# Dilated attention on one NeuronCore: all key groups share one softmax scale before the value products, which then add up with features as rows

## The chip, the core and the metric

The kernel runs on one core of a Trainium2 chip. The core has a matrix engine, TensorE (called PE in the profile, with its weight loads as PEld), a vector engine (DVE), a scalar engine (ACT), GpSimd (POOL) and SyncE (SP), which here does nothing but issue DMAs. Each engine runs its own instructions in order, and semaphores hold an instruction until what it reads is there. The metric is the device time of one execution in microseconds (us).

## The reference, cut to what matters

The model has two layers over 512 tokens of width 1024. Layer 0 mixes latent attention and differential attention, layer 1 mixes dilated attention and stick-breaking attention; a gated convolutional feed-forward block follows each layer. The change lies in the dilated attention of layer 1. It has three groups of four heads of width 64; group g looks back at keys in steps of 1, 4 and 16 tokens. Each group has its own softmax, and the groups are merged by their softmax denominators:

```python
for g, (w, dil) in enumerate(((128, 1), (512, 4), (2048, 16))):
    s = q[g] @ k[g].T * scale - slope * steps          # only the keys of this group's steps
    m = max(s); e = exp(s - m); den = sum(e)
    outs.append((e / den) @ v[g]); lses.append(m + log(den))
wts = softmax(stack(lses), axis=groups)
o = sum_g wts[g] * outs[g]                             # then concatenated and @ w_out
```

Every matmul that feeds from a weight of the model is done as three fp32r products (high times high, high times low, low times high); scores, transposes and value products inside an attention are plain fp32.

## The kernel before, in words

P is 128 and S is 512; the tokens are NT = 4 tiles of 128, and ORDER walks them 3, 2, 1, 0. The function `odd` builds layer 1's mixer. Activations come in as xh and xl, features as rows, tokens as columns.

`proj_T` (the tile apt) makes a 128x512 slice of queries or keys, 24 matmuls of 512 columns (lines 263 to 265, the helper `mm3`), and its result is copied out of PSUM by ACT (L1101, queries) or DVE (L1103, keys). `proj_V` and its `tile_V(i)` (the tile apv) make the values of one token tile, 24 matmuls of 256 columns. Queries and keys of groups 1 and 2 are written in permuted order, so that the tokens of one residue modulo 4 are neighbours: these two groups then need keys of the same residue only, and are handled in four residues r of 128 tokens. Group 0 needs the token tile itself and the one before it.

The dilated attention of groups 1 and 2 is done in units (hp, rp), a pair of heads and a pair of residues. `score12` multiplies queries and keys into two PSUM banks (L1243, a 64-row half of the array for each of the two heads y), DVE adds the bias table and takes the extreme of each row (L1249), and ACT exponentiates and sums the row (L1253). `turn12` transposes the result through PE (L1265) and copies it back (L1267 on ACT, L1269 on DVE). `value12` takes the transposed probabilities as the stationary operand and 64 value columns as the moving one (L1282), and copies the sums, tokens as rows, into `ob` (L1286) with the row sum and the negated maximum beside them. When all units are done, sixteen DMAs (L1295) move `ob` into token order, as `on`.

Group 0 follows in units i of one token tile: `score0` (L1312, L1318, L1321), `turn0` (L1334, L1335, and from L1340 to L1348 the small DVE and ACT steps that turn the two pairs of row sum and maximum into two weights), `value0` (L1359, then L1363 to L1365: the two outputs times their weights, added) and `merged` (L1373: the merged tile is transposed back to features as rows, and split into high and low parts `oG` by L171 on ACT and L172 on DVE).

The helper `skewed` writes these stages one step apart, and puts a projection ahead of each step: the four `proj_T` of group 0 between the units of groups 1 and 2, the four `tile_V` between the units of group 0. The scheduler may then reorder what is written. After it comes the output projection (the tile ao, 24 matmuls of 512 columns for each token tile and the two transposes of normalised tiles, tp L211), whose order is fixed by `tc.manual_schedule`, and then the feed-forward block, which begins with the tile u.

`Weights` loads a weight of 512 KB through the SP queue (L50, tile wraw, three buffers) and splits it on ACT (L72) and DVE (L73). Its `depth` says how many units ahead it is split.

PSUM has eight banks, under five tags: "a" three, "s" two, and "t", "o", "n" one each.

## Time and profile before

| what | value |
|---|---|
| median of 3 runs | 1151.22 us (1151.09 to 1152.02) |
| the profiled execution | 1151.33 us, of which 1149.5 us are the span of the trace |
| PE busy | 1138.7 us |
| DVE busy, ACT busy | 805.6 us, 565.1 us |
| the stage that the change rewrites | from 707.7 us (after the stick-breaking values) to 767.5 us |
| output projection, then feed-forward | from 767.5 us, from 795.4 us |

Times within the trace are counted from the start of its span. A row of a group gives line, engine, operation, the tiles written and read, the shape, a count, the busy time and the mean length of one in ns, and the idle time before it. A row of the timeline gives the start, the length, and then the same names; matmuls are pipelined, so that the length of one overlaps the next and the distance from start to start is its price. Every plain fp32 matmul stands as two records, every fp32r matmul and every transpose as one.

### The profile page before, as it was taken

How to read it: one execution, taken by the hardware profiler on the slowest of the kernel's cores; microseconds unless marked ns; L12 is line 12 of the kernel's file. 1: busy time of each engine (PE TensorE's matmuls, PEld its weight loads, DVE VectorE, ACT ScalarE, POOL GpSimd, SP SyncE). 2: the span in 40 equal slices, each digit the busy share in tenths (PEclk: the TensorE clock that was granted, in tenths of full speed). 3: DMA queues.
4: the chain of work that ended last, by engine and by line, in shares of the span. 5: the costliest groups of instructions: out<-in, count | busy, mean ns of one | idle time of the engine just before them, and what ended most of it. 6: DMA issues, size and time to landing. Idle time of an engine off the chain costs nothing.

```text
span 1149.5 us, 15154 instructions
## 1 busy us (share of the span) xinstructions
PE 1138.7 (99%) x5668; PEld 939.3 (82%) x5668; DVE 805.6 (70%) x1389; ACT 565.1 (49%) x966; POOL 58.0 (5%) x139
## 2 busy tenths in 40 slices
PE   8999999999999999999999999999999999999997
PEld 7876777898888888888888877888988888888886
DVE  6677576467766767899874565577666666679896
ACT  5565566345444444457543464455533433445562
POOL 2100011210000000000030000003000000000002
PEclk9999999999999999999999999999999999999999
DMA  7320421143323332355736223323233323224461
GB/s 278 125 64 1 135 89 50 47 151 114 107 92 92 102 100 83 101 157 164 239 109 179 74 58 106 90 61 113 78 112 105 92 92 103 99 83 140 140 215 74
DMA packets 39050, 126.82 MB, mean 110 GB/s; under 512 B 4672, under 2 KB 6336, under 8 KB 38848
## 3 DMA queue, kind: packets, MB, share of 16 engines
q1 hardware_dynamic: 37056, 122.11, 33.2%
q10 hardware_dynamic: 1920, 3.74, 1.1%
q8 instruction: 45, 0.74, 0.3%
q14 instruction: 29, 0.24, 0.1%
HBM read 117.95 MB, written 6.29 MB: 108 GB/s over the span
## 4 chain that ended last, share of the span: by engine, by line
PE 96%; issue 1%; POOL 1%; DMA 1%; DVE 1%; ACT 0%; SPq 0%; POOLq 0%; DVEq 0%; ACTq 0%
PE u L264 14%; PE u L263 14%; PE u L265 14%; PE acc L263 6%; PE acc L264 6%; PE acc L265 6%; PE apt L263 3%; PE apt L264 3%; PE apt L265 3%; PE ao L263 2%; PE ao L265 2%; PE ao L264 2%; PE sps L773 2%; PE aqk L263 1%; PE av L263 1%; PE aqk L265 1%
## 5 line engine op out<-in xcount | busy, mean ns | idle before, releaser
L73 DVE TENSOR_TENSOR wl<-wraw,wh 128x1024 fp32r<-128x1024 f32 (+1 forms) x202 | 244.5, 1218 | 173.2 <-ACT wh L72 172.5
L72 ACT CAST wh<-wraw 128x1024 fp32r<-128x1024 f32 (+1 forms) x202 | 209.4, 1046 | 277.4 <-PE u L264 179.7
L263 PE MATMUL u<-xh,wh 128*128 128x512 f32 (+1 forms) x768 | 285.5, 372 | 0.0
L264 PE MATMUL u<-xl,wh 128*128 128x512 f32 (+1 forms) x768 | 285.4, 372 | 0.0
L265 PE MATMUL u<-xh,wl 128*128 128x512 f32 (+1 forms) x768 | 285.4, 372 | 0.0
L263 PEld LDWEIGHTS u<-xh,wh 128*128 128x128 f32 x768 | 144.7, 188 | 25.1
L265 PEld LDWEIGHTS u<-xh,wl 128*128 128x128 f32 x768 | 144.7, 188 | 25.1
L264 PEld LDWEIGHTS u<-xl,wh 128*128 128x128 f32 x768 | 144.7, 188 | 24.7
L264 PE MATMUL acc<-wl,gh 128*128 128x512 f32 (+1 forms) x250 | 96.9, 388 | 0.0
L265 PE MATMUL acc<-wh,gl 128*128 128x512 f32 (+1 forms) x250 | 96.9, 388 | 0.0
L263 PE MATMUL acc<-wh,gh 128*128 128x512 f32 (+1 forms) x250 | 96.8, 388 | 0.0
L417 ACT ACTIVATE y<-y 128x512 f32<-128x512 f32 x44 | 27.7, 632 | 85.0 <-DVE y L415 85.0
L412 ACT ACTIVATE y<-u,cw 128x512 f32<-128x512 f32 x88 | 67.4, 774 | 1.7 <-PE u L265 1.7
L415 DVE SCALAR_TENSOR_TENSOR y<-u,cw,y 128x510 f32<-128x510 f32 x88 | 65.6, 747 | 2.5
L413 DVE SCALAR_TENSOR_TENSOR y<-u,cw,y 128x511 f32<-128x511 f32 x88 | 65.1, 743 | 0.9 <-ACT y L412 0.9
L178 POOL TENSOR_TENSOR rv<-ms,epst 128x1 f32<-128x1 f32 x39 | 12.0, 307 | 909.9 <-ACT junk L230 512.3
L263 PEld LDWEIGHTS acc<-wh,gh 128*128 128x128 f32 x250 | 46.9, 188 | 10.1 <-issue 0.6
L265 PEld LDWEIGHTS acc<-wh,gl 128*128 128x128 f32 x250 | 47.0, 188 | 9.6
L264 PEld LDWEIGHTS acc<-wl,gh 128*128 128x128 f32 x250 | 47.0, 188 | 9.5
L263 PE MATMUL apt<-xh,wh 128*128 128x512 f32 x128 | 50.7, 396 | 0.0
L264 PE MATMUL apt<-xl,wh 128*128 128x512 f32 x128 | 50.1, 391 | 0.0
L265 PE MATMUL apt<-xh,wl 128*128 128x512 f32 x128 | 49.9, 390 | 0.0
(324 smaller groups left out, 1902.7 us busy)
## 6 DMA issues: line engine op xcount, KB each, us to landing
wraw<-in_ffn_w_up SPq DMA_DIRECT2D x88, 512.0 KB, 3.6
wraw<-in_ffn_w_down SPq DMA_DIRECT2D x44, 512.0 KB, 3.7
wraw<-in_od_w_dqk SPq DMA_DIRECT2D x12, 512.0 KB, 3.7
wraw<-in_ffn_w_down SPq DMA_DIRECT2D x22, 256.0 KB, 2.6
wraw<-in_ev_w_dqk SPq DMA_DIRECT2D x8, 512.0 KB, 3.9
wraw<-in_ev_w_out SPq DMA_DIRECT2D x8, 512.0 KB, 3.6
spill<-X SPq DMA_DIRECT2D x8, 512.0 KB, 2.6
X<-spill SPq DMA_DIRECT2D x8, 512.0 KB, 6.3
```

The costliest lines, as they stand in the source:

```text
L72: self.nc.scalar.copy(h[:, :w], raw[:, :w])
L73: self.nc.vector.tensor_tensor(l[:, :w], raw[:, :w], h[:, :w].bitcast(F32), ALU.subtract)
L178: POOL.tensor_tensor(v[:, :n], ms, epst[:, :n], ALU.add)
L263: PE.matmul(o, lh, rh, start=first, stop=False, skip_group_check=more)
L264: PE.matmul(o, lh, rl, start=False, stop=False, skip_group_check=more)
L265: PE.matmul(o, ll, rh, start=False, stop=last, skip_group_check=more)
L412: ACT.activation(y[:, z], u, AF.Identity, bias=c[:, 3:4], scale=c[:, 2:3])
L413: DVE.scalar_tensor_tensor(y[:, z, 1:], u[:, :S - 1], c[:, 1:2], y[:, z, 1:], ALU.mult, ALU.add)
L415: DVE.scalar_tensor_tensor(y[:, z, 2:], u[:, :S - 2], c[:, 0:1], y[:, z, 2:], ALU.mult, ALU.add)
L417: ACT.activation(y[:, 0], y[:, 0], AF.Silu)
L773: PE.matmul(s_ps[:, :w], mq[h][:, i * P:(i + 1) * P], mk[h][:, :w], start=True, stop=True)
```

## The change

All three groups get one softmax scale before any value product, and all value products of one pair of heads add up in one PSUM bank.

`score12` and `score0` keep their exponentials in tiles of their own, and write row extreme and row sum into the small tiles `st12` and `st0`. `exchange` moves such a tile (16 KB) through a piece of DRAM, so that the statistics of groups 1 and 2 come to the rows of group 0 (`on`), and those of group 0 to the rows of groups 1 and 2 (`by_r`); each exchange is two DMAs on the SP queue. `share` turns both statistics into one factor for each row and head, for all four tiles at once. `scale0` and `scale12` multiply the exponentials by it, on DVE. `turn0` and `turn12` transpose as before, and ACT alone copies back. `value0` and `value12` now take 64 value columns as the stationary operand and 128 transposed probabilities as the moving one (`add_values`); the output is features as rows, two heads in the two halves of a bank `oT`, and groups 1 and 2 write every fourth column of it. The copies to `ob`, the sixteen DMAs, the products with weights (L1363, L1365) and the transposes of `merged` (L1373) go. Each bank `oT` is split into `oG` once.

The order of the stage is written out under `tc.manual_schedule`: the four `proj_T` with the four `score12`; `tile_V(3)`, `score0(3)`, `tile_V(2)`, `score0` of 2, 1 and 0, `tile_V(1)`, `share`, `tile_V(0)`; then eight steps in each of which a unit is transposed and the unit before it gets its value products. Splits of weights ahead stop before this stage (`W.depth = 0`) and are called by name in steps 3 to 6. Five matmuls of the output projection stand ahead of the last value products in PE's order.

```diff
@@ -1076,8 +1076,11 @@
-                ob = ap.tile([P, 4, 4, 66], F32, tag="ob", name="ob")
-                on = ap.tile([P, NT, 4, 66], F32, tag="on", name="on")
+
+                st0, on = [ap.tile([P, NT, 4, 2], F32, tag=tag, name=tag) for tag in ("st0", "on")]
+                st12, by_r = [ap.tile([P, 4, 4, 2], F32, tag=tag, name=tag) for tag in ("st12", "by_r")]
+                shares = [ap.tile([P, 4, 8], F32, tag=f"share{n}", name="share")[:, :, :4] for n in range(2)]
+                spare = [ap.tile([P, 4, 256], F32, tag=f"spare{n}", name="spare") for n in range(2)]
...
+                    zp = [bank("s", "z12", 2, 2, P) for _ in range(2)]
+                    s = s12[hp, rp] = sb.tile([P, 2, 2, 2, P], F32, tag=("sp", "z")[hp], name="s12", bufs=2)
+                    nm = sb.tile([P, 2, 2], F32, tag="nm12", name="nm12", bufs=2)
...
+                            top_, sum_ = st12[:, r, h, 0:1], st12[:, r, h, 1:2]
                             for g in range(2):
-                                u = 2 * (g + 1) + hp
+                                DVE.tensor_tensor_reduce(
+                                    out=s[:, y, rr, g], in0=zp[y][:, rr, g], in1=tab12[:, g, h], scale=1.0,
+                                    scalar=(3e38 if g == 0 else nm[:, y, rr:rr + 1]), op0=ALU.add, op1=ALU.min,
+                                    accum_out=(nm[:, y, rr:rr + 1] if g == 0 else top_))
+                            ACT.activation(s[:, y, rr], s[:, y, rr], AF.Exp, bias=top_, scale=-1.0, accum_out=sum_)
+
+                tab0 = sb.tile([P, 4, 256], F32, tag="sh", name="tab0")
...
+                def score0(i, banks):
+                    j0, w = span0[i]
+                    z = [bank(t, "z0", 2, 256) for t in banks]
+                    s = s0[i] = [ap.tile([P, 2, 256], F32, tag=f"{'cq' if i > 1 else 'ck'}{2 + 2 * (i % 2) + u}", name="s0")
+                                 for u in range(2)]
...
+                def share(own, other, n, c):
+
+                    own, other = own[:, c], other[:, c]
+                    m, e = [sb.tile([P, k, 4, 4], F32, tag=f"sm{n}{k}", name="sm")[:, :, c] for k in (1, 2)]
+                    DVE.tensor_tensor(m[:, 0], own[:, :, :, 0], other[:, :, :, 0], ALU.min)
+                    for k, st in enumerate((own, other)):
+                        DVE.tensor_tensor(e[:, k], m[:, 0], st[:, :, :, 0], ALU.subtract)
+                    ACT.activation(e, e, AF.Exp)
+                    DVE.tensor_tensor(m[:, 0], e[:, 0], own[:, :, :, 1], ALU.mult)
+                    DVE.tensor_tensor(e[:, 1], e[:, 1], other[:, :, :, 1], ALU.mult)
+                    DVE.tensor_tensor(m[:, 0], m[:, 0], e[:, 1], ALU.add)
+                    DVE.reciprocal(m[:, 0], m[:, 0])
+                    DVE.tensor_tensor(shares[n][:, c], e[:, 0], m[:, 0], ALU.mult)
+
+                def exchange(n, src, dst):
+
+                    d = dpool.tile([S, 8], F32, tag=f"stat{n}", name="stat")
+                    order_ = ("(i q) c -> q i c", "(q r) c -> q r c")
+                    v = [d[:].rearrange("(i q) c -> q i c", i=NT), d[:].rearrange("(q r) c -> q r c", r=4)]
+                    nc.sync.dma_start(v[n], src[:].rearrange("p a b c -> p a (b c)"))
+                    nc.sync.dma_start(dst[:].rearrange("p a b c -> p a (b c)"), v[1 - n])
+
+                begun = set()
+
+                def add_values(u, y, cols, v, p):
+
+                    PE.matmul(oT[u][y * 64:(y + 1) * 64, cols], v, p, start=(u, y) not in begun, stop=True,
+                              skip_group_check=True)
+                    begun.add((u, y))
+
+                def turned_to(n):
+                    tag, pool = (("spare0", ap), ("spare1", ap), ("sl", sb))[n % 3]
+                    return pool.tile([P, 4, 256], F32, tag=tag, name="pt")[:]
+
+                def scale0(i):
+                    for h in range(4):
+                        o = s0[i][h // 2][:, h % 2, :span0[i][1]]
+                        DVE.tensor_scalar(o, o, shares[0][:, i, h:h + 1], None, ALU.mult)
+
+                def turn0(i):
+                    def f():
+                        w = span0[i][1]
+                        pt = turned_to(i)
+                        for u in range(2):
+                            tp = bank(("tn", "aa")[i % 2][u], "t0", 2, 256)
+                            for hh in range(2):
+                                for b in range(0, w, P):
+                                    PE.transpose(tp[:, hh, b:b + P], s0[i][u][:, hh, b:b + P], ident[:])
+                            ACT.copy(pt[:, 2 * u:2 * u + 2, :w], tp[:, :, :w])
+                        return pt
+                    return f
+
+                def value0(i):
+                    def f(pt):
+                        j0, w = span0[i]
+                        for u in range(2):
+                            for b in range(w // P):
                                 for y in range(2):
-                                    rw = slice(y * 64, y * 64 + 64)
-                                    PE.matmul(zp[y][:, rr, g], cq[u][rw, c], ck[u][rw, c], start=True, stop=True)
+                                    h = 2 * u + y
+                                    add_values(u, y, slice(i * P, (i + 1) * P), cv[:, j0 + b, h * 64:(h + 1) * 64],
+                                               pt[:, h, b * P:(b + 1) * P])
+                    return f
+
+                def scale12(hp, rp):
+                    for y in range(2):
+                        for rr in range(2):
+                            o = s12[hp, rp][:, y, rr]
+                            DVE.tensor_scalar(o, o, shares[1][:, 2 * rp + rr, 2 * hp + y:2 * hp + y + 1], None, ALU.mult)
...
+                def turn12(hp, rp):
+                    def f():
+                        s = s12[hp, rp]
+                        pt = turned_to(2 * hp + rp).rearrange("p (y a) (b c) -> p y a b c", y=2, b=2)
...
-                            if y:
-                                ACT.copy(pt[:, y], tp)
-                            else:
-                                DVE.tensor_copy(pt[:, y], tp)
+                            ACT.copy(pt[:, y], tp)
...
-                            o12[hp] = bank("o", "o12", 2, 4, 64)
...
-                                    PE.matmul(o12[hp][:, y, r], pt[:, y, rr, g], cv12[:, r, c:c + 64],
-                                              start=(g == 0), stop=(g == 1))
-                        if rp:
-                            for y in range(2):
-                                DVE.tensor_copy(ob[:, :, 2 * hp + y, 0:64], o12[hp][:, y])
+                                    add_values(hp, y, slice(r, S, 4), cv12[:, r, c:c + 64], pt[:, y, rr, g])
...
-                skewed([[g(hp, rp) for g in (score12, turn12, value12)] for hp in range(2) for rp in range(2)],
-                       fillers)
-                for i in ORDER:
-                    for r in range(4):
-                        nc.sync.dma_start(on[r::4, i], ob[32 * i:32 * i + 32, r])
...
-                tile_V = proj_V(cv)
-                skewed([[g(i) for g in (score0, turn0, value0, merged)] for i in ORDER],
-                       [lambda i=i: tile_V(i) for i in ORDER])
+                W2.depth = 1
...
+                with tc.manual_schedule(engines={PE.engine, DVE.engine, ACT.engine, POOL.engine}):
+                    for n, (x, t) in enumerate((x, t) for x in range(2) for t in (cq, ck)):
+                        proj_T(t[x], (-0.125, 1.0)[t is ck], False, t is cq)
+                        score12(n // 2, n % 2)
+                        if n == 1:
+                            wo2.append(W2.next())
+                    exchange(1, st12, on)
+                    depth, W.depth = W.depth, 0
+                    tile_V = proj_V(cv)
+                    tile_V(3)
+                    score0(3, "ss")
+                    tile_V(2)
+                    score0(2, "tn")
+                    score0(1, "ss")
+                    score0(0, "tn")
+                    tile_V(1)
+                    exchange(0, st0, by_r)
+                    share(st0, on, 0, slice(0, 4))
+                    scale0(3)
+                    scale0(2)
+                    tile_V(0)
+
+                    oT = [bank("so"[k], "oT") for k in range(2)]
+                    oG = [[ap.tile([P, S], F32R, tag=f"{t}{k}", name="og") for k in range(2)] for t in ("cq", "ck")]
+                    todo = [(lambda i=i: scale0(i), turn0(i), value0(i)) for i in ORDER]
+                    todo += [(lambda a=a: scale12(*a), turn12(*a), value12(*a)) for a in ((0, 0), (0, 1), (1, 0), (1, 1))]
+                    pts = {}
+                    for n in range(len(todo) + 1):
+                        if n == 2:
+                            share(st12, by_r, 1, slice(0, 4))
+                        if n + 2 < len(todo):
+                            todo[n + 2][0]()
+                        if n < len(todo):
+                            pts[n] = todo[n][1]()
+                        if n:
+                            todo[n - 1][2](pts.pop(n - 1))
+                        if n == 3:
+                            wo2.append(W2.next())
+                        if n > 3:
+                            W.ahead(W.pos + n - 1 if n < 7 else 0)
+                        if n >= len(todo) - 2 and n != len(todo) - 1:
+                            k = n - len(todo) + 2 >> 1
+                            split(oG[0][k][:], oG[1][k][:], oT[k])
...
+                W.depth = depth
```

More of the change, by code (lines that the diff above doesn't have):

```diff
@@ L1326, in turn0 @@
-                def turn0(i):
-                    def f(s):
-                        w = span0[i][1]
-                        pt = sb.tile([P, 4, 256], F32, tag="sp", name="pt0", bufs=2)
-                        for u in range(2):
-                            tp = bank("tn"[u], "t0", 2, 256)
+                def score0(i, banks):
[5 more added lines that the diff above has]
+                        for hh in range(2):
+                            rw = slice(hh * 64, hh * 64 + 64)
+                            PE.matmul(z[hh][:, u, :w], cq[u][rw, i * P:(i + 1) * P],
+                                      ck[u][rw, j0 * P:(i + 1) * P], start=True, stop=True)
+                    for u in range(2):
+                        for hh in range(2):
+                            h = 2 * u + hh
+                            top_, sum_ = st0[:, i, h, 0:1], st0[:, i, h, 1:2]
+                            o = s[u][:, hh, :w]
+                            DVE.tensor_tensor_reduce(out=o, in0=z[hh][:, u, :w], in1=tab0[:, h, 256 - w:], scale=1.0,
+                                                     scalar=3e38, op0=ALU.add, op1=ALU.min, accum_out=top_)
+                            ACT.activation(o, o, AF.Exp, bias=top_, scale=-1.0, accum_out=sum_)
```

124 lines of the change are left out of this document (25 added, 99 removed).

## The prediction

> **What bounds the kernel now.** I read the page first, busy times, slices and the chain that ended last:
>
> ```profile
> PE 1138.7 (99%) x5668; PEld 939.3 (82%) x5668; DVE 805.6 (70%) x1389; ACT 565.1 (49%) x966; POOL 58.0 (5%) x139
> ...
> PE   8999999999999999999999999999999999999997
> ...
> PE 96%; issue 1%; POOL 1%; DMA 1%; DVE 1%; ACT 0%; SPq 0%; POOLq 0%; DVEq 0%; ACTq 0%
> ```
>
> PE is busy in every slice and is 96% of the chain. So time is gained by taking PE work away and lost by letting PE wait. Then the stretches of the stage, from the end of the stick-breaking values to the feed-forward block, and from there on (length; busy of PE, PEld, DVE, ACT, POOL; clock, DMA share, GB/s):
>
> ```profile
> 707.70:795.40 87.70, 87.70 (x592) 75.97 (x590) 55.54 (x191) 43.61 (x121) 5.50 (x15) 1.00 0.25 79
> 795.40:1149.00 353.60, 347.59 (x1643) 292.08 (x1641) 264.72 (x355) 161.31 (x217) 9.68 (x19) 1.00 0.35 113
> ```
>
> PE idles nowhere in the stage or the output projection, at full clock; the feed-forward behind has its 6 us of idle PE at the very end. What the stage gains or loses therefore reaches the end of the run undiminished. DVE and ACT have room there.
>
> Now the price of each block on PE, from start to start in its timeline:
>
> ```profile
> 713.09 0.39 PE L265 MATMUL apt<-xh,wl 128*128 128x512 f32 x1
> 713.41 1.16 PE L1243 MATMUL z<-ck,cq 64*128 64x128 f32 x16
> 714.50 0.50 PE L263 MATMUL apt<-xh,wh 128*128 128x512 f32 x1
> 714.84 0.39 PE L264 MATMUL apt<-xl,wh 128*128 128x512 f32 x1
> 715.07 0.40 PE L265 MATMUL apt<-xh,wl 128*128 128x512 f32 x1
> ...
> 721.26 1.10 PE L1265 MATMUL t<-ident,s 128*128 128x128 f32 x8
> 722.11 0.47 PE L263 MATMUL apt<-xh,wh 128*128 128x512 f32 x1
> ...
> 729.79 1.90 PE L1282 MATMUL o<-cv,pt 128*128 128x64 f32 x16
> 731.49 0.48 PE L263 MATMUL apt<-xh,wh 128*128 128x512 f32 x1
> 731.81 0.39 PE L264 MATMUL apt<-xl,wh 128*128 128x512 f32 x1
> ```
> ```profile
> 764.20 0.72 PE L1312 MATMUL z<-ck,cq 64*128 64x128 f32 x8
> 764.84 1.09 PE L1334 MATMUL t<-ident,s 128*128 128x128 f32 x8
> ...
> 768.27 0.38 PE L1373 MATMUL tpo<-ident,m 128*128 128x128 f32 x2
> 768.40 0.48 PE L263 MATMUL ao<-wh,osh 128*128 128x512 f32 x1
> ...
> 795.37 0.28 PE L263 MATMUL u<-xh,wh 128*128 128x256 f32 x1
> ```
>
> A 512-column matmul costs 0.23 us (714.84 to 715.07). A value block of 16 records costs 1.70 us (729.79 to 731.49) although it streams only 64 columns each: 0.106 us for a record, as long as a 128-column transpose (0.85 for 8). A score block, which also has 16 records, but of 128 columns and in two halves of the array, costs 1.09 (713.41 to 714.50).
>
> **What goes from PE.** The value products and the transposes of the merged tile:
>
> ```profile
> L1282 PE MATMUL o<-cv,pt 128*128 128x64 f32 x64 | 7.5, 273 | 0.0
> L1359 PE MATMUL o<-cv,pt 128*128 128x64 f32 x56 | 6.7, 271 | 0.0
> L1373 PE MATMUL tpo<-ident,m 128*128 128x128 f32 x8 | 1.6, 278 | 0.0
> ```
>
> 120 records are 7.5 blocks of 1.70, 12.75 us. The matmul behind a block starts its successor 0.32 us later instead of 0.23 (731.49 to 731.81): 0.09 for each of 7 blocks, 0.6. Four pairs of tpo cost 0.13 (768.27 to 768.40) and the same 0.09, 0.9. Together 14.25 us.
>
> **What comes to PE.** Again 120 records, now 128 columns against 64 stationary ones, the two heads alternating between two column halves. The stick-breaking values have this shape; these are their last records, and what follows:
>
> ```profile
> 674.98 0.39 PE L1208 MATMUL osb<-z,sv 128*64 128x128 f32 x4
> ```
> ```profile
> 675.30 0.69 PE L1167 MATMUL zp<-sq,sk 64*128 64x512 f32 x1
> ```
>
> Four records in 0.32 us with the change of array mode at the end; the score block's 1.09 has the same number of records, columns and halves and includes such a change, so I take it, with the 0.09 us lost ahead of it (713.09 and 0.23 to 713.41). Seven blocks of 1.18, and the half block at 0.73 (764.20 to 764.84 is 0.64): 9.0 us. The floor is two heads of 128 columns in a transpose's 0.107 us throughout, 6.4 us; the ceiling is the old pace, 12.75, if the halves do not overlap.
>
> The 60 transposes, the projections and the score products stay. The copies to `ob` and products with weights leave DVE, the scalings come: off the path as long as PE does not wait. To find where it waits I walk the written order, counting from the stage's start at 707.7, with the lengths of these rows:
>
> ```profile
> 749.53 0.42 DVE L1318 CUSTOM_DVE_ANT_0 s<-z,tab 128x256 f32<-128x256 f32 x1 [0.63 <-PE z L1312]
> ...
> 749.88 0.42 DVE L1318 CUSTOM_DVE_ANT_0 s<-z,tab 128x256 f32<-128x256 f32 x1
> ...
> 751.54 0.17 DVE L1340 TENSOR_TENSOR mn<-st,on 128x4 f32<-128x4 f32 x1 [0.55 <-DMA on<-ob]
> ...
> 753.15 0.42 DVE L1363 TENSOR_TENSOR m<-on,wt 128x256 f32<-128x256 f32 x1
> ```
> ```profile
> 750.06 0.51 ACT L1321 ACTIVATE s<-s,st 128x256 f32<-128x256 f32 x1 [6.06 <-DVE st L1318]
> ```
> ```profile
> L777 DVE TENSOR_SCALAR s<-s,rd 128x256 f32<-128x256 f32 x8 | 2.8, 352 | 0.2
> ```
> ```profile
> L1267 ACT COPY pt<-t 128x512 f32<-128x512 f32 x4 | 2.3, 586 | 3.1 <-PE t L1265 3.1
> ```
> ```profile
> L73 DVE TENSOR_TENSOR wl<-wraw,wh 128x1024 fp32r<-128x1024 f32 (+1 forms) x202 | 244.5, 1218 | 173.2 <-ACT wh L72 172.5
> L72 ACT CAST wh<-wraw 128x1024 fp32r<-128x1024 f32 (+1 forms) x202 | 209.4, 1046 | 277.4 <-PE u L264 179.7
> ```
> ```profile
> wraw<-in_ffn_w_up SPq DMA_DIRECT2D x8, 512.0 KB, 3.7
> ...
> spill<-X SPq DMA_DIRECT2D x3, 512.0 KB, 2.6
> on<-ob SPq DMA_DIRECT2D x16, 33.0 KB, 1.9
> ```
>
> Four projections and score blocks end at 27.0 (24 matmuls of 0.23 with their edges, 5.67, and 1.09 each), as before. `tile_V(3)` runs to 30.1 (3.06: 24 matmuls of 256 columns at half of 0.23, and the edges), `score0(3)` to 31.2, `tile_V(2)` to 34.2, `score0(2)` to 35.3, `score0(1)` to 36.2. `score0(0)` takes the banks of `score0(2)`, which DVE reads in four reductions at 0.35 (749.53 to 749.88) from 35.4 on: free at 36.95. PE waits 0.8 us here; the three adjacent score blocks save two mode changes (0.2 each), so +0.4.
>
> `tile_V(1)` and `tile_V(0)` then fill PE until 43.4. Meanwhile ACT does 16 exponentials at 0.5 (750.06; the last four narrower) and has the sums at 41.5. `share` begins at 41.0, when DVE has copied `tile_V(1)`, and takes 1.6 (751.54 to 753.15); its exponential finds ACT free at 41.5, and the first scaled heads are there at 43.3. Transposes start about on time; I charge 0.2 for a scaling that is late at `turn0(2)`. That cover is thin: what delays `share` delays PE one for one.
>
> From here a step costs PE about 2.0 us (0.85 and 1.18), ACT two copies (0.586 each) and in steps 3 to 6 one weight (1.046), DVE four scalings (4 times 0.28: the 0.352 of L777 less the 0.07 by which the reductions overlap) and a weight (1.22, less the same). All fit, with DVE at 2.3 the closest, on a lead of a step or more.
>
> The exchanges go past the SP queue. The first (statistics at 30) has 11 us until `share` and needs two DMAs of 1.9. The second leaves at 41.5 and lands at 45.3 by the 1.9 row, 46.7 at 2.6 each; DVE reaches it at 46.7, behind the scalings, and with 1.6 for the second `share` and 1.1 for four scalings unit (0,0) is ready at 49.5; PE transposes it at 50.0. Cover: 0.5 us. Behind the exchange on SP waits one weight load (3.7), whose split is due at 55.5.
>
> At the end five matmuls of the output projection cover the last copies; the low half of the last `oG` (512 columns: ACT 0.59, DVE half a weight's 1.22) comes 0.25 late by the walk: 0.3 with the extra edges. The sixteen DMAs that go had been waited for 0.55 us by DVE only. The feed-forward finds three split weights at its start as before.
>
> Sum: 14.25 less 9.0, 0.4, 0.2 and 0.3 is 4.35 us gained. Against the profiled execution's 1151.33 us (0.11 over the median of 1151.22) that is **1147.0 us**.
>
> **Rivals.** First, the strided output, which ends on the other side. `value12` writes every fourth column of a bank; no matmul of this trace does. If PSUM takes scattered columns slower, the four blocks of `value12` stretch. For it speaks nothing in the trace; against it that ACT reads PSUM in the same stride at no price, 577 to 591 ns over permuted and plain tiles against 588 to 590 for plain ones:
>
> ```profile
> L1101 ACT ACTIVATE cq<-apt x6: 577/588/591, 651.6 to 728.8; 128x512 f32<-128x512 f32 x6
> L1101 ACT ACTIVATE sq<-apt x2: 588/589/590, 616.5 to 626.8; 128x512 f32<-128x512 f32 x2
> ```
>
> and that an fp32 record streams at half the column rate of an fp32r one already (0.107 us for two overlapping records of 128 against 0.23 for 512). At half pace the four blocks of 0.86 cost 3.4 us more, 1150.4; at a quarter 10.3 more, 1157.3, slower. It decides at a stretch of 2.9 times, where 6.65 us are lost. The Trainium skill (SBUF — State Buffer, Door 1: The DMA port swizzle) has the rule that speaks for it: PSUM works in lines of 8 bytes, and an access that is not contiguous slows matmuls markedly; no run here shows that for a matmul's output.
>
> Second, the halves do not overlap: value blocks at 1.70 and 12.75 instead of 9.0, 1150.7. Against it the osb rows.
>
> Third, PE starves in the written order: no other work stands between a late scaling and PE. If the exchange takes 2.6 and 6.3 us (the page's median for X read back from DRAM) it lands at 50.4, 3.7 late, of which 0.5 is covered: 1150.2. If `share` slips too, or pieces of 32 bytes are slower than these, 2 to 4 us more, 1152 to 1154.
>
> ```profile
> X<-spill SPq DMA_DIRECT2D x8, 512.0 KB, 6.3
> ```
>
> **How the numbers follow.** About 0.2%, 2.3 us, is what a measurement can tell: faster is below 1148.9, slower above 1153.5. Forecast 0.62, between 1144.5 (values at the floor) and 1148.9. Strided at half pace 0.05, same; at a quarter 0.10, slower. No overlap 0.05, same. Starvation 0.18: 0.08 of it same, 0.10 slower. So faster 0.62, same 0.18, slower 0.20. The range leaves out the quarter pace and the worse starvation: 1144.5 to 1152.0.
>
> **What would show it.** `oT` blocks near 1.1 us, alike for `value0` and `value12` (at 1.7: no overlap; `value12` alone long: the stride). PE idle of 0.8 us ahead of `score0(0)`, little ahead of the first transpose of units 0 and (0,0); more there, put down to DVE scalings or to `by_r`, is starvation. The stage and the output projection, 87.7 us now, fall to 83.3. Wrong would be an equal distance, or a feed-forward that is longer than before.

## The result, and the profile after

The changed kernel takes 1147.45 us (median of 6 runs, 1146.87 to 1147.90) against 1151.15 us before (6 runs, 1150.39 to 1152.02): a ratio of 0.9969, with a 95% interval of 0.9959 to 0.9979. The forecast was 1147.0 us, within 1144.5 to 1152.0. The profiled execution took 1147.31 us, of which 1145.2 us are the span.

The page of the changed kernel, its busy times and its chain:

```profile
PE 1134.8 (99%) x5660; PEld 932.1 (81%) x5660; DVE 802.7 (70%) x1375; ACT 568.6 (50%) x966; POOL 57.0 (5%) x139
...
PE 96%; issue 1%; POOL 1%; DVE 1%; DMA 1%; ACT 0%; SPq 0%; POOLq 0%; DVEq 0%; ACTq 0%
```

PE is still the chain; it has 3.9 us less to do (1138.7 less 1134.8), and the run is 3.7 us shorter. The stretches of the changed kernel (length; busy of PE, PEld, DVE, ACT, POOL; clock, DMA share, GB/s):

```profile
707.70:791.10 83.40, 83.06 (x579) 68.38 (x578) 52.80 (x177) 46.34 (x120) 5.24 (x15) 1.00 0.24 77
791.10:1145.00 353.90, 347.83 (x1644) 292.33 (x1643) 264.64 (x355) 161.74 (x217) 8.91 (x19) 1.00 0.36 113
```

The whole gain lies in the rewritten stage and the output projection behind it; the feed-forward keeps its length (353.6 before, 353.9 now, both at full clock). Cut exactly, from the first projection after the stick-breaking values to the first matmul u, the stage and the output projection took 87.63 us before (707.74 to 795.37) and take 84.02 (707.34 to 791.36): 3.61 less. This length, called the stage below, is what the experiments are compared by: the work ahead of it, which no edit touches, ends anywhere between 706.40 and 707.96 in the traces of this case. Each stage is read from one profiled execution; its first part, up to the first value block, takes 45.44 to 45.45 us in the four kernels that share it up to there (the changed one and the first three experiments), so differences of a tenth of a microsecond can be read.

PE's timeline of the changed kernel, at the scores of group 0 and then at the transposes and values:

```profile
741.56 2.00 PE L1270 MATMUL z<-ck,cq 64*128 64x256 f32 x16
743.90 1.05 PE L1270 MATMUL z<-ck,cq 64*128 64x128 f32 x8 [0.34 <-DVE st L1277]
744.88 0.39 PE L263 MATMUL apv<-wh,xh 128*128 128x256 f32 x1
...
750.74 2.11 PE L1328 MATMUL t<-ident,s 128*128 128x128 f32 x16
752.79 1.09 PE L1307 MATMUL oT<-pt,cv 128*64 128x128 f32 x16
753.81 1.09 PE L1328 MATMUL t<-ident,s 128*128 128x128 f32 x8
...
760.11 1.36 PE L1307 MATMUL oT<-pt,cv 128*64 128x128 f32 x16
761.40 1.09 PE L1358 MATMUL t<-ident,s 128*128 128x128 f32 x8
762.42 1.09 PE L1307 MATMUL oT<-pt,cv 128*64 128x128 f32 x16
763.45 1.09 PE L1358 MATMUL t<-ident,s 128*128 128x128 f32 x8
...
766.85 0.43 PE L1307 MATMUL oT<-pt,cv 128*64 128x128 f32 x2
767.21 0.51 PE L265 MATMUL ao<-wh,osl 128*128 128x512 f32 x1
767.64 1.09 PE L1307 MATMUL oT<-pt,cv 128*64 128x128 f32 x14
```

Read from start to start: a value block of 16 records costs 1.02 us, for `value0` (752.79 to 753.81) as for `value12` (762.42 to 763.45), where it cost 1.70. A block of 8 transposes costs 1.02 too (761.40 to 762.42), where it cost 0.85 and 0.09 at its successor. The weight loads idle for 0.17 us ahead of every block from 752.78 to 764.47, as in this row of their timeline in the changed kernel:

```profile
752.78 0.85 PEld L1307 LDWEIGHTS oT<-pt,cv 128*64 128x64 f32 x16 [0.17 <-issue]
```

Nine of these thirteen rows name no releaser, like this one, and the four that name an engine have the same 0.17: it belongs to the change of kind, not to a wait for data.

Three more things stand in PE's rows: PE waits ahead of the third of the adjacent `score0` blocks; the first block of `value12` takes 1.29 (760.11 to 761.40) and none of the later ones does; and the last 16 value records are cut in two by a single matmul of the output projection.

DVE's timeline of the changed kernel where its two shares begin, and ACT's at the two exponentials of the shares and at a later copy:

```profile
748.41 0.17 DVE L1285 TENSOR_TENSOR sm<-st,on 128x16 f32<-128x16 f32 x1
...
750.17 4.03 DVE L1318 TENSOR_SCALAR s<-s,share 128x256 f32<-128x256 f32 x16
754.11 0.17 DVE L1285 TENSOR_TENSOR sm<-st,by_r 128x16 f32<-128x16 f32 x1
```
```profile
748.90 0.23 ACT L1288 ACTIVATE sm<-sm 128x32 f32<-128x32 f32 x1
...
754.61 0.23 ACT L1288 ACTIVATE sm<-sm 128x32 f32<-128x32 f32 x1 [1.13 <-DVE sm L1287]
...
759.25 1.07 ACT L1359 COPY pt<-t 128x512 f32<-128x512 f32 x2 [1.27 <-PE oT L1307]
```

The second share starts at 754.11 straight behind the scalings, with no wait for `by_r`: the last DMA of that exchange starts at 750.58 and lands in 1.6 us, at 752.2, so it lies 1.9 us ready. The last row explains the first block's 1.29 us: ACT's copy waits for PE's values to be done with a buffer. `turned_to(n)` chooses its buffer by n modulo 3, where n is the token tile i for group 0 and 2 hp + rp for the others; unit i = 0 is followed by unit (0,0), so two units in a row get the same one.

### The profile page after: what moved, and what is told of

Read it like the earlier page. It is cut to its first block, busy times and chain, and to the rows that moved or that the text cites. A ratio compares the mean times of both kernels' runs of the same rounds, so it can differ in the third digit from the quotient of the medians.

```text
span 1145.2 us, 15104 instructions
## 1 busy us (share of the span) xinstructions
PE 1134.8 (99%) x5660; PEld 932.1 (81%) x5660; DVE 802.7 (70%) x1375; ACT 568.6 (50%) x966; POOL 57.0 (5%) x139
## 4 chain that ended last, share of the span: by engine, by line
PE 96%; issue 1%; POOL 1%; DVE 1%; DMA 1%; ACT 0%; SPq 0%; POOLq 0%; DVEq 0%; ACTq 0%
PE u L264 14%; PE u L263 14%; PE u L265 14%; PE acc L263 6%; PE acc L265 6%; PE acc L264 6%; PE apt L263 3%; PE apt L264 3%; PE apt L265 3%; PE ao L263 2%; PE ao L265 2%; PE ao L264 2%; PE sps L773 2%; PE aqk L263 1%; PE av L263 1%; PE aqk L265 1%
```

## The experiments

The kernel before, run beside them, took 1151.09 us in the first four comparisons below and 1151.0 us in the others. In brackets behind each time stand its ratio to that and the 95% interval. The changed kernel itself was not run again beside them.

**Values one head after the other.** The two loops over y and over the products change places, so that one head's records stand together.

```diff
-                            for b in range(w // P):
-                                for y in range(2):
+                            for y in range(2):
+                                for b in range(w // P):
...
-                        for rr in range(2):
-                            r = 2 * rp + rr
-                            for g in range(2):
-                                for y in range(2):
+                        for y in range(2):
+                            for rr in range(2):
+                                r = 2 * rp + rr
+                                for g in range(2):
```

> The changed kernel with the value products of the two heads of a pair written one after the other instead of alternating, the same 60 matmuls. Theory (a value block of 16 records takes 1.02 us because records of the two column halves run at the same time): each record then stands alone at 0.107 us, a full block takes 1.71 us and its edges, 7.5 blocks cost 5.2 to 6.4 us more, the time is 1152.5 to 1154, slower than the kernel before. Rival (the block got cheaper because its stationary operand has 64 columns instead of 128, so that loading takes half as long): no change, 1147.5, blocks still at 1.02.

1148.29 us (0.9977, 0.9968 to 0.9986), the stage 85.01. PE's timeline of this kernel:

```profile
752.76 1.15 PE L1307 MATMUL oT<-pt,cv 128*64 128x128 f32 x16
753.83 1.09 PE L1328 MATMUL t<-ident,s 128*128 128x128 f32 x8
...
762.76 1.58 PE L1307 MATMUL oT<-pt,cv 128*64 128x128 f32 x16
764.27 1.09 PE L1358 MATMUL t<-ident,s 128*128 128x128 f32 x8
```

Neither expectation holds. `value0`, where 4 records of one head now follow 4 of the other, costs 1.07; `value12`, with 8 and 8, costs 1.51. The longer `value12` blocks cost 0.5 each, four times; half of these 2 us is hidden, since the 0.27 at the first block of `value12` and the cut in the last one do not appear here. It is not the 5 us that the theory expected: four records of one head in a row still cost nearly what the changed kernel pays. Whether they share it at all is asked again below, with one half of the array only.

**Sums in adjacent columns.** `value12` writes 128 adjacent columns instead of every fourth.

```diff
-                                    add_values(hp, y, slice(r, S, 4), cv12[:, r, c:c + 64], pt[:, y, rr, g])
+                                    add_values(hp, y, slice(r * P, (r + 1) * P), cv12[:, r, c:c + 64], pt[:, y, rr, g])
```

> The changed kernel with groups 1 and 2 writing 128 adjacent columns of the bank instead of every fourth one; the sums then go to the wrong tokens, everything else is as it was. Theory (the stride of the output costs nothing for these fp32 records): value12 blocks stay at 1.02 to 1.03 us, the time stays within 0.3 us of 1147.45. Rival (scattered columns slow a matmul): value12 blocks fall to 0.9 or less and the time by 0.5 us or more.

1148.28 us (0.9976, 0.9967 to 0.9985), outside the 0.3 us that the theory allowed and not below, as the rival had it; the stage 84.01 against 84.02. PE's timeline of this kernel at two blocks of `value12`:

```profile
760.51 1.36 PE L1307 MATMUL oT<-pt,cv 128*64 128x128 f32 x16
761.80 1.09 PE L1358 MATMUL t<-ident,s 128*128 128x128 f32 x8
762.83 1.09 PE L1307 MATMUL oT<-pt,cv 128*64 128x128 f32 x16
763.85 1.09 PE L1358 MATMUL t<-ident,s 128*128 128x128 f32 x8
```

1.29 and 1.02, the same two numbers as with the stride. The stride of four columns costs PE nothing here. That the first block keeps its 1.29 shows that this wait has nothing to do with the columns either. The median is 0.8 us over that of the changed kernel. The stage does not show this, and the profiled execution, at 1147.49 us the third shortest of ten, holds little of it: its span is 0.5 longer, 0.41 of it ahead of the stage, in work that the edit leaves alone. Where the rest of the 0.8 us comes from stays open.

**A late exchange.** The statistics of group 0 take three more DMAs from DRAM to DRAM on their way.

```diff
+                    for hop in range(3 if n == 0 else 0):
+                        e = dpool.tile([S, 8], F32, tag=f"hop{hop}", name="hop")
+                        nc.sync.dma_start(e[:], d[:])
+                        d = e
+                    v = [d[:].rearrange("(i q) c -> q i c", i=NT), d[:].rearrange("(q r) c -> q r c", r=4)]
```

> The changed kernel with three more copies from DRAM to DRAM between the two DMAs of the second exchange, which carries the statistics of group 0 to the rows of groups 1 and 2. Each should take about 1.8 us from issue to the next issue, as the write of the exchange does, so by_r lands some 5.4 us later. Theory (nothing stands between a late scaling and PE in the written order): DVE covers 1.9 us and the first transpose of groups 1 and 2 another 0.5, the rest reaches PE: 3.0 us idle ahead of that transpose, 1150.5, up to 1151.5 when a copy takes 2.1. Rival (the order has work enough to take up a late exchange): under 1 us more.

1150.05 us (0.9996, 0.9987 to 1.0005), the stage 86.27, so 2.25 more, where the theory had 3.0 and 1150.5 and the rival under 1. DVE, ACT and PE of this kernel, where they wait:

```profile
758.15 0.18 DVE L1285 TENSOR_TENSOR sm<-st,by_r 128x16 f32<-128x16 f32 x1 [4.24 <-DMA by_r<-hop]
```
```profile
758.66 0.23 ACT L1288 ACTIVATE sm<-sm 128x32 f32<-128x32 f32 x1 [5.46 <-DVE sm L1287]
758.80 1.60 ACT L1334 COPY pt<-t 128x512 f32<-128x512 f32 x4
```
```profile
759.42 1.15 PE L1312 MATMUL oT<-pt,cv 128*64 128x128 f32 x16 [1.79 <-ACT pt L1334]
760.49 1.09 PE L1363 MATMUL t<-ident,s 128*128 128x128 f32 x8
```

`by_r` came at 758.15 instead of 752.2, 6.2 us later counted from the stage's start (707.06 here, 707.34 there), and PE's first transpose of unit (0,0) at 760.49 instead of 757.47, 3.3 later: some 2.9 us of an exchange's delay are covered. The rest is the starvation that the prediction feared, and this run shows that it is real. Its place is not the one that the theory named, the transposes of unit (0,0). The share's exponential stands in ACT's queue ahead of the copies of `turn0(1)`, so that values of group 0, which need nothing of this exchange, wait behind it. PE spent 1.4 us of the gap on six matmuls of the output projection, and idled 1.79.

**Three waits taken away.** `score0(0)` takes other banks, the turned tiles go round by a count of their own, and at the end of the stage the first split of `oT` moves behind the last copies of transposed probabilities and the third weight behind both splits. PE's own order is not edited there; the planner then lets the last values run through, with the output projection behind them.

```diff
-                    tag, pool = (("spare0", ap), ("spare1", ap), ("sl", sb))[n % 3]
+                    turns_made.append(n)
+                    tag, pool = (("spare0", ap), ("spare1", ap), ("sl", sb))[len(turns_made) % 3]
...
-                    score0(0, "tn")
+                    score0(0, "to")
...
-                        if n > 3:
-                            W.ahead(W.pos + n - 1 if n < 7 else 0)
-                        if n >= len(todo) - 2 and n != len(todo) - 1:
-                            k = n - len(todo) + 2 >> 1
+                        if n in (4, 5):
+                            W.ahead(W.pos + n - 1)
+                        if n >= len(todo) - 1:
+                            k = n - len(todo) + 1
...
+                    W.ahead(W.pos + 5)
```

> The changed kernel without the four waits that its trace shows: score0(0) takes the banks t and o, which are free, in place of those of score0(2); the three tiles for transposed probabilities are used in turn (now two units in a row use the same one); the first split of oT comes after the last copies of transposed probabilities; the third weight split of the stage comes at its end. Theory: 0.8 us at score0(0), 0.27 at the first value12, and about 0.6 of the 0.75 at the end come back, 1.3 to 1.7 us, 1145.9 (1145.6 to 1146.4). Rival (each wait that goes uncovers the next one behind it, the scaling, so that nothing is gained): 1147.2 to 1147.5, with the idle time now ahead of the first transposes.

1145.82 us (0.9958, 0.9945 to 0.9970), the stage 82.25: 1.77 less than the changed kernel. The first block of `value12` now costs 1.03 (759.79 to 760.82), so the buffer was its cause. The stage's first transpose comes only 0.3 earlier, since `score0(0)` still shares the bank "t" with `score0(2)`: of the banks that the expectation called free, only "o" is. Most of the gain lies at the end, where the last 32 value records now run through:

```profile
763.89 1.97 PE L1307 MATMUL oT<-pt,cv 128*64 128x128 f32 x32
```

**Other banks and the buffers, without the end.** This takes the banks "o" and "a", which are free at that time, and leaves the text of the end as the changed kernel has it.

```diff
-                    tag, pool = (("spare0", ap), ("spare1", ap), ("sl", sb))[n % 3]
+                    turns_made.append(n)
+                    tag, pool = (("spare0", ap), ("spare1", ap), ("sl", sb))[len(turns_made) % 3]
...
-                    score0(0, "tn")
+                    score0(0, "oa")
```

> The changed kernel with two edits: score0(0) takes the free banks o and a instead of those that score0(2) fills, and the turned tiles go round by their own count. Theory: the 0.8 us ahead of score0(0) is a wait for the reductions of score0(2), and the 0.27 us at the first values of heads in groups 1 and 2 a wait for a tile; both go, and with them 1.0 us: stage plus output projection 83.0 instead of 84.02, 1146.3 to 1146.8, and no idle time of PE ahead of z0(0). Rival: PE waits there for DVE's reductions whatever the banks (DVE is the bound around the scores of group 0), and the idle time moves to the next block that needs a bank: 83.7 to 84.0, 1147.2 or more.

1146.14 us (0.9963, 0.9949 to 0.9976), the stage 83.19, 0.83 less: between the two expectations. PE's timeline of this kernel, then DVE's and ACT's:

```profile
740.62 2.44 PE L1270 MATMUL z<-ck,cq 64*128 64x256 f32 x24
742.99 0.39 PE L263 MATMUL apv<-wh,xh 128*128 128x256 f32 x1
...
749.41 2.28 PE L1331 MATMUL t<-ident,s 128*128 128x128 f32 x16 [0.40 <-DVE s L1321]
```
```profile
748.00 0.18 DVE L1289 TENSOR_TENSOR sm<-sm,st 128x16 f32<-128x16 f32 x1 [1.02 <-ACT sm L1288]
```
```profile
747.75 0.21 ACT L1288 ACTIVATE sm<-sm 128x32 f32<-128x32 f32 x1
```

The three score blocks take 2.37 us instead of 3.32, so the wait for banks was 0.95. But most of it comes back at the first transposes: they begin 0.56 late for the work ahead of them (749.41 less 742.99 is 6.42, 5.86 in the changed kernel), 0.40 of it the wait in their row, and their block takes 2.21 instead of 2.05. The first value block comes 0.23 earlier than in the changed kernel. ACT's sixteen exponentials end at the same time after the stage's start as in the changed kernel (747.75 less 706.40 is 41.35; the share's exponential there started at 41.56), and now DVE's share waits 1.02 for them and PE for the scaling. So both expectations were half right: the wait for banks is gone, and ACT is the next that is late. The kernel above has its first value block at the same place (45.22 us after the stage's start in both), so the 0.94 by which its stage is shorter (83.19 less 82.25) is what the interleaved end costs here. It is not quite the end of the changed kernel: there the planner puts five matmuls of the output projection ahead of the last 16 value records, here one.

**Two units a step.** The same banks and buffers, values behind one another at the end, and the transposes of two units put together, then the values of two.

```diff
-                    score0(0, "tn")
+                    score0(0, "oa")
...
-                    for n in range(len(todo) + 1):
...
+                    turned_(0)
...
+                    turned_(1)
+                    valued(0)
+                    share(st12, by_r, 1, slice(0, 4))
...
+                    turned_(2)
...
+                    turned_(3)
+                    valued(1)
+                    valued(2)
...
+                    turned_(4)
...
+                    turned_(5)
+                    valued(3)
+                    valued(4)
+                    W.ahead(W.pos + 3)
+                    turned_(6)
+                    turned_(7)
+                    valued(5)
+                    half(0)
+                    valued(6)
+                    valued(7)
+                    half(1)
+                    W.ahead(W.pos + 5)
```

> The changed kernel with the stage's last part in another order: the transposes of two units stand together, and then the values of two units, so that PE changes between the two kinds of block 8 times instead of 16; score0(0) takes the free banks o and a, the turned tiles go round by their own count, and oT is split behind all values of its pair. Theory: each change of kind costs 0.17 us, seen as the weight load's own idle ahead of every block in the trace of the changed kernel, so eight fewer give 1.4 us on top of the 1.77 us that the stage without its waits gained: stage plus output projection 80.9 instead of 84.02 us, and 1144.3 to 1145.0. Rival: the steps of 1.02 us are set by the records themselves (0.107 each with their overlap) and the change of kind is free; then blocks side by side show no gain and the stage stays at 82.3, 1145.6 to 1146.

1145.08 us (0.9953, 0.9941 to 0.9966), the lowest median of all, and the stage 81.37, between the 80.9 and the 82.3 of the two expectations. PE's timeline of this kernel:

```profile
750.97 2.27 PE L1331 MATMUL t<-ident,s 128*128 128x128 f32 x16 [0.40 <-DVE s L1321]
753.17 1.09 PE L1307 MATMUL oT<-pt,cv 128*64 128x128 f32 x16
754.20 1.53 PE L1331 MATMUL t<-ident,s 128*128 128x128 f32 x12
755.66 1.97 PE L1307 MATMUL oT<-pt,cv 128*64 128x128 f32 x32
757.56 1.97 PE L1361 MATMUL t<-ident,s 128*128 128x128 f32 x16
759.45 1.53 PE L1307 MATMUL oT<-pt,cv 128*64 128x128 f32 x24
760.92 1.97 PE L1361 MATMUL t<-ident,s 128*128 128x128 f32 x16
762.81 2.84 PE L1307 MATMUL oT<-pt,cv 128*64 128x128 f32 x48
765.58 0.50 PE L263 MATMUL ao<-wh,osh 128*128 128x512 f32 x1
```

Here the price of a record and that of a change of kind come apart. 16 value records cost 1.02, 32 cost 1.90, 48 cost 2.77: 0.055 for a record, and 0.14 for each block whatever its length. 8 transposes cost 1.02, 16 cost 1.89: 0.109 and 0.15. The expectation had 16 changes and 0.17 each; the kernel with an undisturbed end has 14 and this one 8, and the stage is 0.88 shorter (82.25 less 81.37), 0.15 for each of the six. That is why the gain stays under the one expected: eight changes at 0.17 were counted, six at 0.15 went. The late scaling has no part in it, since the first value block comes at 45.21 us, as in the kernel without the waits.

**One half of the array only.** Both heads of a pair are put in the same half, so that no two records can share the array.

```diff
-                    PE.matmul(oT[u][y * 64:(y + 1) * 64, cols], v, p, start=(u, y) not in begun, stop=True,
-                              skip_group_check=True)
+                    if u not in begun:
+                        PE.matmul(oT[u], oS[0][:, 0, :P], oS[0][:, 0], start=True, stop=True, skip_group_check=True)
+                        begun.add(u)
+                    PE.matmul(oT[u][:64, cols], v, p, start=False, stop=True, skip_group_check=True)
```

> The changed kernel with both heads of a pair written to the same 64 columns of the array and the same rows of the sum (the head of the upper half is added to that of the lower one, so the sums hold something else; the count, sizes and order of the value records stay, and two wide matmuls of 0.23 us clear the sums first). Theory: the changed kernel's 1.02 us for 16 records comes from two halves that run at the same time; with one half alone a record of 128 columns costs about 0.107, a block 1.7, and the 7.5 blocks 5.1 us more with the two clears: stage plus output projection 89.1 to 90.5, and 1152 to 1153.5. Rival: what was gained comes from the 64 stationary columns (half the array to load for each record), whichever half they stand in: blocks of 1.02, and 1147.5 to 1148.

1153.01 us (1.0018, 1.0009 to 1.0027), the stage 89.78: 5.76 more, inside the theory's range. PE's timeline of this kernel:

```profile
766.57 1.96 PE L1310 MATMUL oT<-pt,cv 128*64 128x128 f32 x16
768.46 1.09 PE L1360 MATMUL t<-ident,s 128*128 128x128 f32 x8
769.48 3.71 PE L1310 MATMUL oT<-pt,cv 128*64 128x128 f32 x32
773.12 0.50 PE L263 MATMUL ao<-wh,osh 128*128 128x512 f32 x1
```

16 records cost 1.89 and 32 cost 3.64: 0.109 for a record, twice the 0.055 of two halves and about the old 0.106. A stationary operand of 64 columns alone saves nothing. For 120 records that is 6.5 us. The two clears take 1.0 more, twice what was expected: the first 16 records and the clears last 2.86 us (752.29 to 755.15) instead of 1.89. Both together are the 7.5 by which this stage is longer than that of the kernel without the waits (89.78 less 82.25); against the changed kernel it is less, because the 0.27 and the cut at the end are absent here too. In this run the two heads also add to the same sums; that this is not what slows them is argued and not shown: a transpose, which adds to nothing, costs the same 0.109 us a record. So without the halves working at the same time nothing of the gain is left: the stage less the clears is 88.8 us, 1.2 more than before the change.

**No written order.** The stage without `tc.manual_schedule`; the planner then orders the same text.

```diff
-                with tc.manual_schedule(engines={PE.engine, DVE.engine, ACT.engine, POOL.engine}):
+                if True:
```

> The changed kernel without the written order around the stage: the planner orders its instructions. Theory: PE's order stays that of the text but for the output projection, which no longer stands between the last values, and the time is decided by PE's blocks: 1146.6 to 1147.9. Rival: the written order holds DVE's scalings and shares ahead of other work; a planner that puts weights or splits ahead of them delays the transposes of units 0 and (0,0): over 1148.5, with idle PE put down to DVE scalings.

1146.86 us (0.9966, 0.9952 to 0.9979), the stage 83.38. As the theory had it: PE's blocks come in the order of the text, and the last 32 value records run through. The rival's mechanism is there too, but small: PE waits 0.21 us for it. DVE's timeline of this kernel shows a weight inside the second share, and PE's the wait that follows:

```profile
755.97 1.22 DVE L73 TENSOR_TENSOR wl<-wraw,wh 128x1024 fp32r<-128x1024 f32 x1
757.11 0.17 DVE L1289 TENSOR_TENSOR sm<-sm,st 128x16 f32<-128x16 f32 x1
```
```profile
758.51 1.24 PE L1358 MATMUL t<-ident,s 128*128 128x128 f32 x8 [0.21 <-DVE s L1348]
```

So the written order is not what the change gains by.

## Why the prediction was right, and by how much

The sum gave 4.35 us; the stage shows 3.61 and the medians 3.70. By the steps of the prediction:

- **The bound.** PE is the chain and the stage's gain reaches the end undiminished: right, the feed-forward kept its length.
- **The values and the steps.** A step was costed at 2.03 (0.85 for transposes and 1.18 for values) and takes 2.04 (1.02 and 1.02). The sum was right, its split was not. The price of a change of kind falls on both kinds of block; the prediction gave the values two edges and the transposes none. Without the changes, 120 records at 0.055 are 6.6 us, near the floor of 6.4. The Trainium skill (TensorEngine Tiling (Array Packing), Key Properties) states that tiles run in parallel and that a change of the tiling mode drains TensorE. The rows agree with the first, at 0.055 against 0.109 us; for the second they show that a change has a price, 0.14 us, and not that it is a drain. Between kinds that both use the whole array a change was not free either, some 0.06 to 0.09 us in the kernel before (8 transposes ahead of an old value block took 0.93, from 728.86 to 729.79, and 8 at 0.109 are 0.87). How much of the 0.14 is the halves' own is not separated.
- **The walk to the first transpose.** It was put at 43.4 us after the stage's start and is at 43.40 (750.74 less 707.34). The wait ahead of `score0(0)` was put at 0.8; taking it away shortened that place by 0.95, and moved the first value block by only 0.23, since ACT and the scaling are late behind it. The share began at 41.07 for 41.0. The late scaling, 0.2, shows as the first 16 transposes, which take 2.05 where 16 cost 1.89 elsewhere.
- **The exchange.** It landed at 44.9 (752.2), before the 45.3 to 46.7 forecast, DVE reached it at 46.77 for 46.7, and unit (0,0) was transposed at 50.13 for 50.0. The cover of 0.5 was reckoned from the late end of that range; the late exchange measured 2.9, which is the 1.9 that `by_r` lay ready and 1.0 behind it.
- **The end** is the term that was mis-sized: 0.3 charged, 1.27 found. From the first value block to the first matmul u the changed kernel takes 38.57 us (752.79 to 791.36) and the kernel without the waits 37.03 (752.47 to 789.50); 0.27 of the 1.54 between them is the buffer's. The walk looked for the late copy of the last `oG` and counted "the extra edges" as small. But from 765.49 to 768.66 six matmuls of the output projection (0.23 each) and 16 value records (0.055 each) take 3.17 us where their own prices add up to 2.26: 0.9 for the changes between them. The rest, some 0.3, are gaps in front of the first matmuls that read `oG`, of which this row of the weight loads' timeline in the changed kernel shows the longest:

```profile
770.13 0.19 PEld L265 LDWEIGHTS ao<-wo,og 128*128 128x128 f32 x1 [0.43 <-DVE og L172]
```

- **A wait that no step had.** 0.27 us at the first block of `value12`, from two units in a row with the same buffer. The walk let units follow each other through three buffers and did not count the index where group 0 ends.

Taking 0.97 at the end and 0.27 at the buffer from 4.35 leaves 3.1, and 3.61 were measured: something was gained that the sum did not have. Most of it can be named, as an estimate. The sum took the 0.09 us at a block's successor off for the old values and the merged transposes, but not for the transposes that stay. In the kernel before, five pieces of these stand ahead of a projection matmul (at 722.11, 741.82, 742.50, 754.41 and 771.33), 0.4 us together, and in the changed kernel none does; the last 0.1 is not accounted for. So the mechanism was foreseen, but that the time came within 0.45 us of the forecast is in part luck: errors of 1.2 one way and 0.5 the other.

The rivals. The strided output as a cost is refuted: its blocks take 1.02 as the others do, and adjacent columns change neither them nor the stage. The rule of the Trainium skill that spoke for it stands also in PSUM — Partial Sum Buffer, Specifications (TRN2); the measurement decides against it for plain fp32 records that write every fourth column. No overlap is refuted for the kernel as it is, and its price is shown: 5.76 us when it is forced, which makes the kernel slower than before. The prediction had it at 3.75 (12.75 less 9.0), because it gave values without overlap the old blocks of 1.70 with no price for the change of kind; the rows have 1.89, and the clears are in the 5.76. Starvation did not occur, and is shown to be possible: an exchange that is 6 us late takes 2.25 of the stage's 3.61 us away.

What stays open is how far apart records of the two halves may stand. With 2, 4 and 8 records of one head in a row a block of 16 costs 1.02, 1.07 and 1.51, and 1.89 in one half. It fits these numbers within 0.06 if each half can hold some three records that wait while PE's order goes on: a run of 8 then delays the other half by about 5 records, 5 times 0.109 on top of 0.88 and 0.14, which is 1.57, and a run of 4 by one, 1.13. No run looked at that directly.

## What to carry to other kernels

When a matmul's moving side has 64 columns, make it the stationary one and let two of them stand in the two column halves: that halves the price of a record as long as the two halves' records are mixed finely. In runs of 8 more than half of that was gone (1.51 us for a block, between 1.02 and 1.89), and in one half alone all of it. Once PE runs one short block after another, count its changes of kind: each cost 0.14 us here, and grouping two units for each kind took 0.88 us off the stage. Before writing an order out, walk the buffers' indices through every seam between two loops, and look for what stands behind an exchange in each engine's queue, also where it belongs to other work.

## What the runs showed of the hardware

- A change between transposes and values in column halves costs PE 0.14 to 0.15 us in either direction, with 0.17 us of idle weight loads and no wait for data.
- Two column halves share the array without strict alternation: 4 records of each in turn cost 1.07, 8 and 8 cost 1.51, where strict pairs cost 1.02 and one half alone 1.89.
- Plain fp32 matmuls write every fourth column of a PSUM bank at the price of adjacent ones, 1.02 us for 16 records in both.
- The DMA that reads the 16 KB of `by_r` back from DRAM, 128 adjacent bytes for each row, lands in 1.6 us, earlier than any other group of this kernel's DMA issues; `on`, 16 KB in pieces of 32 bytes, takes 1.9.
